# LayerNorm with GELU: giving each partition one stretch of 512 KB in memory instead of 32 KB of every 4 MB block

## The chip, the cores and the metric

One core of one Trainium2 chip runs the kernel; the other cores are idle. The time is the device time in microseconds (us).

## The reference

`x` is 8 x 1024 x 2048 float32: 8192 rows of 2048 numbers, 8 KB a row, 64 MB in all. The output has the same size.

```python
mean = np.mean(x, axis=-1, keepdims=True)
var = np.var(x, axis=-1, keepdims=True)
out = gamma * ((x - mean) / np.sqrt(var + eps)) + beta
return 0.5 * out * (1 + np.tanh(np.sqrt(2 / np.pi) * (out + 0.044715 * out ** 3)))
```

Every row is handled by itself, so any row may be given to any partition, as long as its result is stored in the row it came from.

## The kernel before

The rows are cut into B = 16 blocks of 4 MB. A block gives each of the 128 partitions R = 4 rows, 32 KB. Five slots in SBUF hold a block each; the result is written over the input in its slot and stored from there.

```python
R = 4
SLOTS = 5
SPLIT = 3
...
xg = xf.rearrange("(b p r) d -> b p r d", p=P, r=R)     # block, partition, row
og = of.rearrange("(b p r) d -> b p r d", p=P, r=R)
...
@block.sync                                              # loads
def _(sy):
    for b in range(B):
        s = slot(b)
        if stored(b):
            sy.wait_ge(s_store[s], stored(b))            # the slot's last store has landed
        for q in range(R):
            if b == 0:                                   # blocks 0 and SPLIT: four loads of 1 MB
                sy.dma_start(out=xts[s][:, q:q + 1], in_=xg[0, :, q:q + 1]).then_inc(s_first[q], 16)
            elif b == SPLIT:
                sy.dma_start(out=xts[s][:, q:q + 1], in_=xg[b, :, q:q + 1]).then_inc(s_load[s], 16)
        if b not in (0, SPLIT):
            sy.dma_start(out=xts[s], in_=xg[b]).then_inc(s_load[s], 16 * R)
...                                                      # in the scalar engine's loop over rows:
    if by_row(b):                                        # the last block is stored row by row
        ...
        ac.dma_start(out=og[b, :, q:q + 1], in_=xt[:, q:q + 1])...
    elif q == R - 1:
        ins.then_inc(s_r, 1)
        ac.dma_start(out=og[b], in_=xt)._wait_ge(s_r, b + 1).then_inc(s_store[slot(b)], 16)
```

VectorE takes the statistics, GpSimd the reciprocal root, ScalarE the scaling, VectorE the product with gamma, TensorE adds beta, ScalarE applies GELU.

## Time and profile before

| | before |
|---|---|
| time, median | 320.19 us (320.02 to 320.31, 3 runs) |
| span of the profiled run | 318.5 us |
| bytes moved | 134.26 MB, 421 GB/s on average |
| busiest compute engine (ScalarE) | 79% |
| the two DMA queues together | 98.4% of 16 engines' span |
| 32 KB load packets | 1792, mean 1214.5 ns, 13 of them over 1240 ns |
| 32 KB store packets | 1920, mean 1214.8 ns |

How to read it: the sum of the queue shares says whether the DMA engines have time left, and here they have next to none (98.4%). A share of busy time does not tell whether the engines move data at full pace while they are busy: in one stretch of the changed kernel, shown below, a DMA share of 1.03 stands beside 303 GB/s. For that one looks at the GB/s column of a table of stretches, and at the durations of single packets in the trace. The numbers of packets and their durations in this document are counted from those packet records; a packet is one 32 KB piece of one partition unless its size is given. The table of stretches credits a whole packet to the stretch in which it starts, so in a stretch of 4 us one packet of 32 KB more or less is 8 GB/s.

Two views of before are kept here for later comparison. First, the table of stretches for the 3.7 us before the first store starts, for the 4 us in which the first store ends and the second starts, and for the long middle (columns: window, length, PE, PEld, DVE, ACT, POOL busy, clock, DMA share, GB/s):

```profile
36.00:39.70 3.70, 3.26 (x8) 0.68 (x6) 3.13 (x6) 3.12 (x2) 1.71 (x5) 1.00 1.03 363
53.00:57.00 4.00, 3.27 (x8) 0.70 (x7) 3.43 (x7) 4.00 (x3) 1.63 (x3) 1.00 0.99 426
60.00:260.00 200.00, 160.65 (x349) 37.16 (x348) 165.58 (x262) 165.82 (x88) 74.99 (x132) 1.00 1.00 433
```

Second, the DMA pieces of the chain that ended last, in order of time (start us, us, what):

```profile
68.79 26.55 DMA out_dram<-xt
95.35 33.54 DMA xt<-in_x_dram
...
215.78 35.01 DMA out_dram<-xt
250.80 34.20 DMA xt<-in_x_dram
```

### The profile page before, as it was taken

What the parts mean: (1) busy time and instruction counts of PE and PEld (TensorE: products, weight loads), DVE (VectorE), ACT (ScalarE), POOL (GpSimd) and SP (SyncE); (2) the same over time, 40 slices, a digit from 0 to 9 for tenths busy, and PEclk for the clock granted to TensorE, in tenths of its full rate; (3) what the DMA queues carried; (4) which work ended last, traced back from release to release, by engine and by line L of the source; (5) the groups of instructions that cost most, each with busy time, mean ns of one, the idle gap of its engine ahead of it and who ended that gap; (6) DMA issues with size and microseconds to landing.
All of it is one profiled execution on the core that took longest, in us unless ns stands there. A gap on an engine that the chain in (4) does not pass through costs nothing.

```text
span 318.5 us, 2090 instructions
## 1 busy us (share of the span) xinstructions
PE 244.3 (77%) x520; PEld 57.2 (18%) x520; DVE 247.5 (78%) x386; ACT 251.7 (79%) x132; POOL 110.6 (35%) x201
## 2 busy tenths in 40 slices
PE   2769999999999989687795868958589595886860
PEld 1212222222212112111121112212112121111110
DVE  3499999999999897786968968599686986869810
ACT  2769999999999989698696967969589695995970
POOL 1144444444444444232443333333332433324300
DMA  7999999999999999999999999999999999999995
GB/s 289 438 457 401 394 434 430 444 424 436 432 424 444 417 453 416 440 440 416 457 403 457 420 436 444 411 461 403 453 432 424 449 407 457 424 432 403 453 396 209
DMA packets 6002, 134.26 MB, mean 421 GB/s; under 512 B 704, under 2 KB 752, under 8 KB 752
## 3 DMA queue, kind: packets, MB, share of 16 engines
q1 hardware_dynamic: 3168, 67.11, 49.4%
q10 hardware_dynamic: 2832, 67.13, 49.0%
q14 instruction: 2, 0.02, 0.0%
HBM read 67.13 MB, written 67.11 MB: 421 GB/s over the span
## 4 chain that ended last, share of the span: by engine, by line
DMA 64%; ACT 14%; DVE 10%; POOL 5%; PE 3%; issue 1%; ACTq 0%; DVEq 0%; POOLq 0%; SPq 0%
DMA xt<-in_x_dram 32%; DMA out_dram<-xt 30%; ACT yk L195 9%; DVE sts L149 7%; ACT xt L202 4%; POOL ves L135 3%; DVE zg L158 2%; PE ps L220 2%; DMA rows<-in_gamma_dram 2%; POOL rss L137 2%; POOL nms L139 1%; DVE mvs L155 1%; PE ps L237 1%; ACT g_t L191 1%; ACTq L205 0%
## 5 line engine op out<-in xcount | busy, mean ns | idle before, releaser
L149 DVE BATCH_NORM_STATS2 sts<-xt 128x6 f32<-128x512 f32 x256 | 157.7, 679 | 33.5 <-DMA xt<-in_x_dram 31.9
L195 ACT ACTIVATE yk<-xt,nms,rss 128x2048 bf16<-128x2048 f32 x64 | 133.7, 2090 | 48.9 <-POOL nms L139 42.9
L237 PE MATMUL ps<-zg,ident 128*128 128x512 bf16 x256 | 120.8, 627 | 55.8 <-DVE zg L158 54.7
L233 PE MATMUL ps<-b_hl,ones_b 33*128 33x512 bf16 x256 | 120.6, 624 | 2.2 <-PEq L228 2.2
L202 ACT ACTIVATE xt<-ps 128x2048 f32<-128x2048 f32 x64 | 118.9, 1858 | 1.5 <-PE ps L237 1.5
L135 POOL TENSOR_SCALAR ves<-mvs 128x1 f32<-128x1 f32 x64 | 38.5, 602 | 179.2 <-DVE mvs L155 179.2
L158 DVE TENSOR_TENSOR zg<-yk,g_t 128x2048 bf16<-128x2048 bf16 x64 | 76.5, 1195 | 19.2 <-ACT yk L195 19.2
L237 PEld LDWEIGHTS ps<-zg,ident 128*128 128x128 bf16 x256 | 27.6, 130 | 149.0 <-DVE zg L158 113.7
L233 PEld LDWEIGHTS ps<-b_hl,ones_b 33*128 33x128 bf16 x256 | 27.0, 127 | 92.1 <-issue 88.4
L139 POOL TENSOR_SCALAR nms<-mvs,rss 128x1 f32<-128x1 f32 x64 | 35.7, 558 | 6.3
L137 POOL TENSOR_TENSOR rss<-ves,mhalf 128x1 f32<-128x1 f32 x64 | 35.3, 552 | 5.3
L155 DVE BATCH_NORM_AGGREGATE mvs<-sts 128x2 f32<-128x24 f32 x64 | 16.9, 264 | 2.2
L220 PE MATMUL ps<-rows,ones 1*128 1x512 f32 x8 | 7.2, 1076 | 6.1 <-DMA rows<-in_gamma_dram 6.1
L188 ACT ACTIVATE b_hl<-rows 1x2048 bf16<-1x2048 f32 x1 | 1.9, 1909 | 5.3 <-DMA rows<-in_beta_dram 5.3
L166 DVE TENSOR_TENSOR b_hl<-rows,b_hl 1x2048 bf16<-1x2048 f32 x1 | 2.3, 2280 | 2.8 <-ACT b_hl L189 2.8
L220 PEld LDWEIGHTS ps<-rows,ones 1*128 1x128 f32 x8 | 2.5, 327 | 9.2 <-DMA rows<-in_gamma_dram 6.1
L191 ACT ACTIVATE g_t<-ps 128x2048 bf16<-128x2048 f32 x1 | 1.9, 1877 | 1.9 <-PE ps L220 1.9
L184 ACT ACT_TABLE_LOAD x1 | 1.3, 1283 | 0.9 <-SPq L107 0.9
L189 ACT ACTIVATE b_hl<-rows 1x2048 bf16<-1x2048 f32 x1 | 1.9, 1908 | 0.0
L161 DVE MEMSET b_hl<- 33x1024 uint32 x1 | 0.9, 912 | 1.2 <-SPq L107 1.2
L126 POOL MEMSET ones<- 65x128 f32 x1 | 0.2, 202 | 0.5 <-SPq L107 0.5
L130 POOL TENSOR_SCALAR_AFFINE_SELECT ident<-ident 128x128 bf16<-128x128 bf16 x1 | 0.3, 295 | 0.1
(7 smaller groups left out, 0.9 us busy)
## 6 DMA issues: line engine op xcount, KB each, us to landing
out_dram<-xt ACTq DMA_DIRECT2D x15, 4096.0 KB, 32.6
xt<-in_x_dram SPq DMA_DIRECT2D x14, 4096.0 KB
xt<-in_x_dram SPq DMA_DIRECT2D x8, 1024.0 KB, 8.4
out_dram<-xt ACTq DMA_DIRECT2D x4, 1024.0 KB, 8.6
rows<-in_beta_dram ACTq DMA_DIRECT2D x2, 8.0 KB, 5.9
rows<-in_gamma_dram ACTq DMA_DIRECT2D x1, 8.0 KB, 5.1
```

Source lines behind the costliest of these rows:

```text
L135: po.tensor_scalar(out=ves[:, c], in0=mvs[:, k, 1:2], scalar1=float(eps), scalar2=1.0, op0=ALU.add, op1=ALU.mult)._wait_ge(s_a, k + 1).the ...
L137: po.tensor_tensor(out=rss[:, c], in0=ves[:, c], in1=mhalf, op=ALU.pow)._wait_ge(s_q, 2 * k + 1).then_inc(s_q, 1)
L139: po.tensor_scalar(out=nms[:, c], in0=mvs[:, k, 0:1], scalar1=rss[:, c], scalar2=-1.0, op0=ALU.mult, op1=ALU.mult)._wait_ge(s_q, 2 * k + 2 ...
L149: ins = ve.bn_stats(out=sts[:, q, j, :], in_=xr[:, j, :])
L155: ve.bn_aggr(out=mvs[:, q], in_=sts[:, q])._wait_ge(s_o, count).then_inc(s_a, 1)
L158: ve.tensor_tensor(out=zgs[q % 2], in0=yks[q % 2], in1=g_t, op=ALU.mult)._wait_ge(s_n, count).then_inc(s_z, 1)
L191: ac.activation(out=g_t, in_=pss[0], func=ACT.Identity)._wait_ge(s_tg, 1).then_inc(s_c, 1)
L195: ac.activation(out=yks[t % 2], in_=xts[slot(b)][:, q], func=ACT.Identity, scale=rss[:, q:q + 1], bias=nms[:, q:q + 1])._wait_ge(s_p, t + ...
L202: ins = ac.activation(out=xt[:, q], in_=pss[i % 2], func=ACT.Gelu_apprx_tanh)._wait_ge(s_t, i + 1)
L220: ins = pe.matmul(pss[0][:, cols(j)], lhsT=ones[64:65], rhs=rows[64:65, j * K // nsub:(j + 1) * K // nsub, :d // K], start=True, stop=True)
L233: ins = pe.matmul(ps[:, cols(j)], lhsT=ones_b, rhs=b_hl[:, cols(j)], start=True, stop=False)
L237: ins = pe.matmul(ps[:, cols(j)], lhsT=ident, rhs=zgs[k % 2][:, cols(j)], start=False, stop=True)
```

## The change

Each partition takes one stretch of 64 consecutive rows, 512 KB. Block b is the b-th 32 KB of every stretch. The intent is plain from the pattern: each partition then walks through memory in order. The 128 pieces of one transfer now lie 512 KB apart and not side by side.

```diff
-    xg = xf.rearrange("(b p r) d -> b p r d", p=P, r=R)
-    og = of.rearrange("(b p r) d -> b p r d", p=P, r=R)
+
+    xg = xf.rearrange("(p b r) d -> b p r d", p=P, r=R)
+    og = of.rearrange("(p b r) d -> b p r d", p=P, r=R)
```

## The prediction

> **What bounds the kernel now.** I read the page from its top: the span, the slices, the queue shares. Then the chain that ended last, the waits of the load queue, and a table of stretches.
>
> From the page of the kernel before, span, engine shares, slices and queues:
>
> ```profile
> span 318.5 us, 2090 instructions
> PE 244.3 (77%) x520; PEld 57.2 (18%) x520; DVE 247.5 (78%) x386; ACT 251.7 (79%) x132; POOL 110.6 (35%) x201
> ...
> DMA  7999999999999999999999999999999999999995
> ...
> DMA packets 6002, 134.26 MB, mean 421 GB/s; under 512 B 704, under 2 KB 752, under 8 KB 752
> ...
> q1 hardware_dynamic: 3168, 67.11, 49.4%
> q10 hardware_dynamic: 2832, 67.13, 49.0%
> ```
>
> The reader is to see that no compute engine is over 79% busy, while the DMA digits are 9 from the second slice to the last but one. The two queues (q1 loads, q10 stores) together hold the 16 DMA engines for 49.4 + 49.0 = 98.4% of 318.5 us, that is 313.4 us per engine. The DMA engines have no idle time to give.
>
> The chain that ended last, and the load queue's own waits:
>
> ```profile
> DMA 64%; ACT 14%; DVE 10%; POOL 5%; PE 3%; issue 1%; ACTq 0%; DVEq 0%; POOLq 0%; SPq 0%
> ...
> SPq L122 <- DMA out_dram<-xt: 240.3, 11, 47.2
> ```
>
> The chain is DMA for 64%, loads and stores in turn. The load queue spends 240.3 us waiting for stores to empty a slot: load b+5 goes out when store b lands. So loads and stores form one loop through five slots, and a store that lands late makes a load late. The 36% of the chain put down to compute lies mostly where the engines still have queued packets from other slots: in those stretches the DMA digits are still 9.
>
> The table of stretches (us; the last two columns are the share of the DMA engines' time and the rate):
>
> ```profile
> 20.00:60.00 40.00, 36.14 (x79) 8.25 (x77) 36.99 (x60) 37.46 (x20) 16.61 (x29) 1.00 1.00 421
> 60.00:100.00 40.00, 36.08 (x80) 8.41 (x80) 36.99 (x61) 37.06 (x21) 16.46 (x30) 1.00 1.00 433
> 140.00:180.00 40.00, 30.65 (x67) 6.94 (x65) 31.22 (x49) 31.69 (x18) 14.56 (x27) 1.00 1.00 433
> 220.00:260.00 40.00, 30.59 (x68) 7.14 (x66) 31.50 (x51) 31.58 (x18) 13.73 (x24) 1.00 1.00 432
> 290.00:318.50 28.50, 15.71 (x35) 3.42 (x32) 11.78 (x18) 17.30 (x9) 4.69 (x9) 1.00 0.84 354
> ```
>
> The rate is 432 to 433 GB/s in every middle stretch, whether only loads run (20 to 40 us) or loads and stores together. That flatness is the main reading. The packet records behind it say the same: a 32 KB load packet has a median of 1213 ns (tenth percentile 1213, ninetieth 1218), a 32 KB store packet a median of 1213 and a ninetieth percentile of 1215. 32768 B / 1213 ns = 27.0 GB/s per engine, times 16 is 432 GB/s. A memory that stalls now and then would spread these durations; there is no spread. [...]
>
> [...]
>
> [...]
>
> [...]
>
> [...]
>
> **The change, part by part.** Only the order of the row index differs: partition p's rows in block b were rows b*512 + 4p to b*512 + 4p + 3, and become p*64 + 4b to p*64 + 4b + 3. Same permutation for input and output, and every row is normalised by itself, so the result stays right.
>
> Removed: a 4 MB block that is contiguous in memory (partition pitch 32 KB). Added: a block of 128 pieces of 32 KB at a pitch of 16 blocks x 32 KB = 512 KB. Moved: nothing in SBUF; partition p receives the same 32 KB tile shape in the same slot[...].
>
> Unchanged: the number of packets. Loads: 14 transfers x 128 pieces of 32 KB = 1792, plus 8 x 128 = 1024 of 8 KB. Stores: 15 x 128 = 1920 of 32 KB, plus 4 x 128 = 512 of 8 KB. [...]Issue cost, semaphores, waits and all compute instructions stay too. So instruction costs add 0 us, and the whole question is the duration of a packet.
>
> The sum per engine now. 32 KB packets: (1792 + 1920) / 16 = 232 x 1.215 us (mean of both kinds) = 281.9 us. 8 KB packets: 1024 / 16 x 0.331 + 512 / 16 x 0.314 = 21.2 + 10.0 = 31.2 us. Together 313.1, against 313.4 from the shares. The remaining 5.4 us of the span are the first 1.9 us before a packet starts and the holes of the tail, where the last stores wait for compute (0.84 busy from 290 on: 0.16 x 28.5 = 4.6 us). These are fixed. So span = 5.4 + 313.1 x f, where f is the lengthening of a packet, and the time is the span plus 1.7 us (320.19 against 318.5).
>
> Nothing hides a lengthening: at 98.4% busy it goes to the end nearly in full. One limit on that is the tail: if the memory is slower, compute has more slack, but its holes come after the last load and stay. Slower by 2% is 6.4 us, so f = 1.0205, a 32 KB packet of 1.24 us for 1.215.
>
> **Rivals.** (a) No effect: [...]f = 1.000, time 320. For it: packets without spread[...]. Against it: [...]the flatness promises nothing about another address pattern.
>
> (b) [...]
>
> (c) [...]loads and stores meet: slots put the load about four or five blocks ahead of the store, only 128 to 160 KB within the same partition's stretch, if the two tensors start at like addresses. [...]I give this whole tail, over 340 us, 6%.
>
> (d) One engine slower than the rest: a transfer's semaphore fills when the last of 16 has landed[...].
>
> (e) Faster: packets are at their minimum (1211 ns smallest, 1213 median), and start and tail holes do not depend on addresses. If all 8 KB packets reached a quarter of 1213, 303 ns, that would save 313.1 - 281.9 - 96 x 0.303 = 2.1 us, 0.7%. Faster by 2% cannot be reached: 1%.
>
> **Range and chances.** I weigh (a) with small losses up to 2% at 0.57, (b) and its neighbours from 327 to 340 at 0.36, (c) at 0.06. The median of this lies where a loss of about 1.2% stands: 313.1 x 0.012 = 3.8 us, so 324. The low end is the kernel before less half a microsecond's gain, 319[...]. Faster 0.01, within 2% 0.57, slower 0.42.
>
> **What would show it.** If (a): queue shares again 49.4 and 49.0, middle stretches at 432 to 433 GB/s, 32 KB packets at 1213 ns without spread. If (b): the same counts of packets, shares still near 98 to 99% of a longer span, but [...]a wider spread of packet times; the loads-only stretch from 20 to 40 us tells whether reads alone suffer. If (c): under 400 GB/s where loads and stores overlap. If (d): the DMA share falls below 0.97 in the middle stretches while single packets stay short. In every case compute groups should keep their mean durations (statistics 679 ns, scaling 2090 ns, last activation 1858 ns) and only idle time grow. The prediction is wrong in its ground if packet counts change, if a compute group lengthens, or if the time falls under 314.

The sum came to 5.4 + 313.1 x 1.012 = 322.3 us of span and so to a time of 324 us, with a range of 319 to 336. Terms of it are cut above, since no trace or run of this case shows what they rested on: rival (b), by which every packet is longer (weighed at 327 to 340 us), the high end of the range, which was built on (b), the time that (c) was worked out to, and the cost named for (d). The 1.2% is only the author's estimate, the median of the chances that are given.

## The result, and the profile after

The changed kernel took 324.28 us (median of 4 runs, 323.57 to 324.62) against 320.2 us. Ratio 1.0125, 95% interval 1.0107 to 1.0143. A ratio here is the mean time of one kernel's runs over the mean of the other's of the same rounds, so it is not quite the ratio of the medians. Executions over 1.5% slower than the fastest of the same kernel are left out of the means. In the terms of the prediction this is "within 2%", and it is slower beyond doubt.

From the page after, span and queues:

```profile
span 322.6 us, 2090 instructions
...
q1 hardware_dynamic: 3168, 67.11, 49.7%
q10 hardware_dynamic: 2832, 67.13, 48.4%
```

Same instructions, same packets. The load queue's share rose on a longer span: 0.497 x 322.6 = 160.3 us per engine against 0.494 x 318.5 = 157.3. The store queue's did not: 156.1 us both times. So the loads became slower and the stores did not.

The stretches of after that answer to those shown of before:

```profile
20.00:60.00 40.00, 36.17 (x79) 8.27 (x77) 37.01 (x59) 37.37 (x20) 16.58 (x29) 1.00 1.01 412
60.00:100.00 40.00, 36.12 (x79) 8.38 (x79) 37.02 (x61) 37.10 (x21) 16.46 (x30) 1.00 1.00 429
140.00:180.00 40.00, 30.54 (x67) 7.18 (x68) 31.46 (x50) 31.05 (x17) 13.73 (x25) 1.00 1.00 431
220.00:260.00 40.00, 29.82 (x65) 6.83 (x64) 30.73 (x50) 30.81 (x17) 13.69 (x24) 1.00 1.01 429
290.00:322.60 32.60, 16.70 (x36) 3.84 (x36) 16.29 (x25) 18.45 (x10) 6.52 (x12) 1.00 0.83 352
```

The rate went from 432 or 433 to 429 to 431 GB/s in the middle, and from 421 to 412 between 20 and 60 us. The DMA share stays at 1.00: the engines are as occupied as before and move less. The loss between 20 and 60 us has a place. The same 4 us as above, and the same middle, now of after:

```profile
53.00:57.00 4.00, 3.28 (x9) 0.70 (x8) 3.44 (x7) 3.96 (x3) 1.63 (x4) 1.00 1.03 303
60.00:260.00 200.00, 157.47 (x341) 36.26 (x340) 162.06 (x257) 161.96 (x86) 73.13 (x129) 1.00 1.00 430
```

In the 4 us, 426 became 303 GB/s. The packet records say what fills them: the first store's last packets have just gone out, the second store's first packet comes at 57.1 us, and in between all 16 engines work on loads. Those packets take up to 2755 ns for 1213. Counted over the whole run:

| 32 KB load packets | before | after |
|---|---|---|
| mean | 1214.5 ns | 1240.4 ns |
| median | 1213 ns | 1213 ns |
| over 1240 ns | 13 | 145 |
| before the first store is issued, over 1240 ns | 0 of 256 | 0 of 256 |
| later, with under 2 of 16 engines on stores, over 1240 ns | 0 of 200 | 37 of 62 |
| within 3 us of a handover, over 1240 ns | 1 of 763 | 141 of 720 |
| 32 KB store packets, mean | 1214.8 ns | 1214.6 ns |

(Engines on stores: the mean number of store packets under way while the load packet ran. A packet counts as within 3 us when any part of it is.) So a load packet is not slower in general. A few are slow, where one store ends and the next begins; I call the time from the last packet of one store to the first of the next a handover below, and there are 14 of them. Of all the time that 32 KB load packets take over 1213 ns, 97% lies within 3 us of one: the slow ones between 192 and 196 us, for instance, stand around a store whose last packets end at 193.4 us. The 32 KB loads that start before any store is issued (12 to 31 us) are untouched.

The 8 KB loads just ahead of the first store are not, and in neither kernel. Of the 8 KB load packets that start between 36 us, when the first store is issued, and its first packet at 39.8 us, 33 of 166 take over 400 ns in before and 23 of 178 in after, against a mean of 314 and 313 ns in the 3 us ahead of that. The longest take 840 and 1048 ns, and all the slow ones start in the last 1.5 us. So the kernel before knows this stall too, before any store packet moves; the 363 GB/s of its line for 36.00 to 39.70 above show it, and after has 392 in the same stretch.

The chain of after has the same pieces in the same order, a little later each:

```profile
68.85 28.82 DMA out_dram<-xt
97.69 33.86 DMA xt<-in_x_dram
...
218.91 36.21 DMA out_dram<-xt
255.13 34.41 DMA xt<-in_x_dram
```

The six long DMA pieces of the chain sum to 198.4 us before (26.55 + 33.54 + 34.99 + 34.07 + 35.01 + 34.20) and to 202.8 after (28.82 + 33.86 + 35.00 + 34.52 + 36.21 + 34.41). The 4.4 us are the whole difference of the spans (4.1 us) within the noise of one trace; what follows the last load takes 33.5 us before and 33.1 after.

The 145 slow packets do not explain all of that. All packet time over 16 engines is 313.7 us before and 316.5 after: 2.8 us. The remaining 1.3 us I put down to unevenness; no run isolates it. A transfer is done when the last of its 16 engines has landed, and the trace records each landing. From the first to the last landing of one 4 MB store it is 1.5 us at the first of those I could separate and 2.7 at the most before; after, it grows through the run: 2.1, 2.5, 2.4, 2.5, 2.8, 3.4, 3.9, 4.3, 5.4, 5.5, 5.5, and 1.9 for the last one, when loads are over. Why the landings draw apart is not shown; the trace does not name engines.

### The profile page after: what moved, and what is told of

It reads as the page before. It is cut to its first block, busy times and chain, and to the rows that moved or that the text cites. A ratio compares the mean times of both kernels' runs of the same rounds, so it can differ in the third digit from the quotient of the medians.

```text
span 322.6 us, 2090 instructions
## 1 busy us (share of the span) xinstructions
PE 244.3 (76%) x520; PEld 57.1 (18%) x520; DVE 247.3 (77%) x386; ACT 251.7 (78%) x132; POOL 110.0 (34%) x201
## 2 busy tenths in 40 slices
DMA packets 6002, 134.26 MB, mean 416 GB/s; under 512 B 704, under 2 KB 752, under 8 KB 752
## 4 chain that ended last, share of the span: by engine, by line
DMA 64%; ACT 13%; DVE 10%; POOL 5%; PE 3%; issue 1%; ACTq 0%; DVEq 0%; POOLq 0%; SPq 0%
DMA xt<-in_x_dram 32%; DMA out_dram<-xt 31%; ACT yk L196 8%; DVE sts L150 7%; ACT xt L203 4%; POOL ves L136 3%; DVE zg L159 2%; PE ps L221 2%; DMA rows<-in_gamma_dram 2%; POOL rss L138 2%; POOL nms L140 1%; DVE mvs L156 1%; PE ps L238 1%; ACT g_t L192 1%; ACTq L206 0%
## 5 line engine op out<-in xcount | busy, mean ns | idle before, releaser
L196 ACT ACTIVATE yk<-xt,nms,rss 128x2048 bf16<-128x2048 f32 x64 | 133.7, 2089 | 53.4 <-POOL nms L140 47.4
L203 ACT ACTIVATE xt<-ps 128x2048 f32<-128x2048 f32 x64 | 118.9, 1858 | 1.5 <-PE ps L238 1.5
```

The lines of the kernel that those rows point to most:

```text
L196: ac.activation(out=yks[t % 2], in_=xts[slot(b)][:, q], func=ACT.Identity, scale=rss[:, q:q + 1], bias=nms[:, q:q + 1])._wait_ge(s_p, t + ...
L203: ins = ac.activation(out=xt[:, q], in_=pss[i % 2], func=ACT.Gelu_apprx_tanh)._wait_ge(s_t, i + 1)
```

## The experiments

All three theories that I began with accept the table above and differ in what makes a read slow at a handover. R: strided reads by themselves. W: strided writes, behind which reads wait. C: loads and stores that work in the same stretches, 128 to 160 KB apart. Results first; every row is told below.

| run | time, median us | ratio to before, 95% | slow 32 KB loads | load mean ns | packet time per engine us |
|---|---|---|---|---|---|
| before | 320.2 | 1 | 13 of 1792 | 1214.5 | 313.7 |
| after | 324.28 | 1.0125 (1.0107 to 1.0143) | 145 of 1792 | 1240.4 | 316.5 |
| after_again | 323.19 | 1.0091 (1.0066 to 1.0116) | 134 of 1792 | 1239.5 | 316.4 |
| x_strided | 321.96 | 1.0048 (1.0028 to 1.0068) | 100 of 1792 | 1228.9 | 315.3 |
| out_strided | 321.4 | 1.005 (1.0025 to 1.0076) | 80 of 1792 | 1224.0 | 314.7 |
| pitch256 | 320.75 | 1.003 (1.0005 to 1.0055) | 37 of 1792 | 1215.7 | 314.1 |
| pitch64 | 320.32 | 1.0003 (0.9989 to 1.0016) | 58 of 1792 | 1217.5 | 314.0 |
| pitch504 | 327.87 | 1.0254 (1.0227 to 1.028) | 41 of 1664 | 1217.6 | 314.0 |
| pitch504b | 319.84 | 0.9982 (0.997 to 0.9995) | 8 of 1792 | 1214.8 | 313.2 |

The last three columns belong to the one profiled run of each kernel. Its time was 324.45 us for after, 323.87 for after_again, 323.25 for x_strided, 321.16 for out_strided, 320.19 for pitch256 and 327.71 for pitch504, which is not always near the median. Five more runs (near, near_contig, half_stores and its control, odd_cut) are told below without a row, as their packets or their course differ too much.

### One side at a time: x_strided and out_strided

```diff
 # x_strided: the loads as in the changed kernel, the stores as before
-    og = of.rearrange("(p b r) d -> b p r d", p=P, r=R)
+    og = of.rearrange("(b p r) d -> b p r d", p=P, r=R)
 # out_strided: the other way round
-    xg = xf.rearrange("(p b r) d -> b p r d", p=P, r=R)
+    xg = xf.rearrange("(b p r) d -> b p r d", p=P, r=R)
```

Both put rows in wrong places; their timing is what is wanted.

> Only the loads take the 512 KB pitch; the stores keep the contiguous 4 MB block (the result is wrong on purpose: rows come out permuted). Theory R (strided reads stall by themselves whenever all 16 engines read at once): the full loss, 324 us, some 145 of the 1792 large load packets over 1240 ns, mean near 1240. Theory C (a load and a store collide because both work in the same 512 KB stretches, 128 to 160 KB apart): loads and stores are now in unrelated patterns, so 320 us and under 30 slow load packets. Theory W (scattered writes keep the memory busy and reads behind them wait): 320 us, no slow packets.

> Only the stores take the 512 KB pitch; the loads keep the contiguous block (wrong on purpose). Theory R: 320 us, load packets at 1213 to 1215 ns. Theory C: 320 us. Theory W: the full loss, 324 us, load packets slow in the 2 to 4 us between two stores, store packets still 1213.

Neither expectation came true as written. Each side alone costs about half a per cent, 1.5 us, both together 3 to 4 us. The first handover of each, x_strided and then out_strided:

```profile
53.00:57.00 4.00, 3.27 (x9) 0.70 (x7) 3.43 (x7) 4.00 (x3) 1.63 (x3) 1.00 1.06 377
```

```profile
53.00:57.00 4.00, 3.27 (x8) 0.71 (x7) 3.43 (x6) 3.77 (x3) 1.83 (x4) 1.00 1.07 393
```

377 and 393 GB/s, where before has 426 and the full change 303. The two are only two packets apart. Summed from the packet records, the time over 1213 ns of load packets that start between 50 and 62 us says the same: 0.04 us per engine before, 0.76 and 0.67 with one side strided, 1.33 with both. C falls as the whole cause: with one side strided there are no common stretches, and the stalls are there. R and W fall as sole causes: each side alone brings stalls. What fits is that the pitch of either side makes a read at a handover more likely to wait (100 and 80 slow loads for 13). In out_strided the loads have the very addresses of the kernel before, and 80 of them are slow for 13; so it is not a matter of the read's own address alone. Even then only loads lengthen: the stores' mean is 1214.3 ns.

### A smaller pitch: pitch256 and pitch64

```diff
-    xg = xf.rearrange("(p b r) d -> b p r d", p=P, r=R)
+    xv = xf.rearrange("(g p b r) d -> g b p r d", g=2, p=P, r=R)     # pitch64: g=8
+    xg = [xv[b // 8, b % 8] for b in range(B)]                       # pitch64: b // 2, b % 2
 # and the same for the output
```

> Loads and stores both with half the pitch, 256 KB (two groups of eight blocks; the result is right). If the loss comes from large powers of two between engines and shrinks with the pitch: 321 to 322.5 us, load packets at a mean of 1220 to 1230 ns. If any pitch that is not contiguous costs the same (collision within one stretch[...]): 324 us.

> Pitch 64 KB, eight groups of two blocks, so a transfer spreads over 8 MB and no longer lies in one piece. Power-of-two theory: 320 to 320.5 us, no slow packets, since the kernel before has 32 KB and none. If non-contiguity itself costs: still above 322 us.

The loss falls from 1.25% to 0.3% at half the pitch (320.75 us, less than the 321 to 322.5 expected), and to nothing at 64 KB, which still is no contiguous block. So scattering as such is not what costs. The counts of slow packets do not fall evenly (37 at 256 KB, 58 at 64 KB where none were expected; they are mild, with means of 1215.7 and 1217.5 ns), and the profiled run at 256 KB was one of 320.19 us, without the loss that three of the six runs show (321.23 to 322.56). So I read no law of the pitch from them.

### The same chip for what follows: after_again

No edit; the changed kernel once more.

> The changed kernel once more, on the chip of the three runs beside it, as their yardstick: 1.010 to 1.014 of the kernel before, 323.5 to 324.6 us, load packets with a mean near 1240 ns, store packets at 1215.

1.0091, a little under what was expected, with the same 2.7 us of added packet time (316.4). The first-store handover costs 1.33 us per engine in it, as it did the first time: nearly half of the excess of all 32 KB loads over 1213 ns (2.96 us) lies in one handover of 14.

### Another order of the same stretches: near, and its control near_contig

```diff
 # near: partition 8j+i takes stretch 16i+j, still 512 KB each, still in steps of 32 KB
-    xg = xf.rearrange("(p b r) d -> b p r d", p=P, r=R)
+    xv = xf.rearrange("(i j b r) d -> b j i (r d)", i=8, j=16, r=R)
 # near_contig: the same two-level pattern inside contiguous blocks
+    xv = xf.rearrange("(b i j r) d -> b j i (r d)", i=8, j=16, r=R)
 # and the same for the row-wise loads and for the output
```

> Each partition keeps one 512 KB stretch, in steps of 32 KB, for loads and stores; but stretches are dealt to partitions in another order (partition 8j+i has stretch 16i+j)[...]. Right result. Theory D (what counts is the distance between engines that work at the same moment): nearly as pitch 256, 320 to 321.5 us, under 60 slow load packets. Theory S (what counts is that a partition stays in one stretch and steps by 32 KB, whoever works beside it): 324 us as the changed kernel.

> Control for the run of 423 us: the same two-level address pattern and the same order of partitions, but inside the contiguous 4 MB blocks of the kernel before, so no large power of two in the addresses. If the 423 us came from memory addresses: near 320 us and 430 GB/s in the loads-only stretch. If they came from the way in which a two-level pattern is dealt to the DMA engines[...]: near 420 us, and about 215 GB/s in the loads-only stretch.

Near took 422.82 us, 32% more (1.3158 to 1.324 without the one slow run of six), which no theory of mine had; a stretch of loads alone shows little over half of the 406 GB/s that before has there (near):

```profile
20.00:40.00 20.00, 11.11 (x24) 2.56 (x24) 8.84 (x14) 11.46 (x6) 5.33 (x9) 1.00 1.06 221
```

Taken by itself this run would have looked like a spectacular proof that the addresses are to blame. The control, whose addresses are all inside contiguous blocks, took 423.27 us with the same rate (near_contig):

```profile
20.00:40.00 20.00, 11.12 (x24) 2.58 (x24) 8.96 (x15) 11.46 (x6) 5.33 (x9) 1.00 1.09 227
```

So the large power of two in the addresses has nothing to do with it. Shown is that loads alone ran at 221 and 227 GB/s with this two-level pattern on the memory side, 16 outer and 8 inner, for 406 in before, with addresses far apart or in one block. The reason is not shown: the trace does not name engines. Near therefore says nothing about the change, and the question of which engines' distance matters stays open.

### Closing the handovers: half_stores and before_half_stores

```diff
-                    elif q == R - 1:
+                    elif q % 2 == 1:
                         ins.then_inc(s_r, 1)
-                        ac.dma_start(out=og[b], in_=xt)._wait_ge(s_r, b + 1)...
+                        ac.dma_start(out=og[b, :, q - 1:q + 1], in_=xt[:, q - 1:q + 1])._wait_ge(s_r, 2 * b + (q + 1) // 2)...
 # before_half_stores: the same edit in the kernel before
```

> The changed kernel with each 4 MB store cut into two of 2 MB (16 KB per partition), the first issued two rows earlier, so the store queue should not run dry between two blocks. Theory G (reads stall in the gap of 2 to 4 us when no store is under way and all 16 engines read): gaps gone, slow load packets fall from 145 to under 50, and most of the 4 us comes back: 320.5 to 322 us. If the stalls come from loads and stores being under way together, which this increases: 324 us or more.

> The same cut of the stores in the kernel before, as control: it has no stalls to remove and is at 98 per cent of its DMA engines, so 319.5 to 320.8 us.

A miss: 328.84 us (ratio 1.0252, 1.0229 to 1.0275) and 327.0 us for the control (1.022, 1.0181 to 1.0259; against a mark of 2% that is unclear, but slower it is). Both are slower than what they came from, so the pair doesn't test what it was made for. Slow load packets did not fall to under 50 but rose, to 213, and the control, expected to have no stalls, has 106 of them, many far from its first store; the time over 1213 ns is 4.6 and 2.2 us per engine. The cut also changed how the two queues share the rate: loads run at some 290 GB/s beside stores at 145 (60 to 120 us), which is the ratio of their pieces, 32 and 16 KB. In before, with 32 KB on both sides, it is 216 and 216 (60 to 260 us). One thing is worth keeping from the control. Its first store is issued at 27.8 us, while loads run at full pace, and starts at 33.1 us. The stretches ahead of and within that time (before_half_stores):

```profile
24.00:29.00 5.00, 4.95 (x12) 1.12 (x10) 4.97 (x10) 4.42 (x4) 1.85 (x3) 1.00 0.97 419
29.40:33.00 3.60, 2.88 (x8) 0.73 (x6) 3.04 (x6) 3.60 (x3) 1.62 (x3) 1.00 0.99 282
```

Loads of the contiguous layout fall from 419 to 282 GB/s while a store starts up behind them, with no earlier store anywhere. The stall is therefore not made by the pitch; it exists in the layout of before too. The kernel before itself shows it in the 8 KB loads ahead of its first store (363 GB/s, above), while its first handover is clean (426). That it goes with the start of the store, and not with 8 KB loads as such, the control shows too: its first store starts 6.6 us earlier, and of its 64 load packets of 8 KB that start between 36 and 39.8 us none takes over 309 ns.

### Long stretches without stores: odd_cut

```diff
-                        ac.dma_start(out=og[b], in_=xt)._wait_ge(s_r, b + 1)...
+                        w = P if b % 2 == 0 else 16
+                        ac.dma_start(out=og[b, :w], in_=xt[:w])._wait_ge(s_r, b + 1)...
```

Most rows of odd blocks stay unwritten, so the result is wrong.

> The changed kernel with the stores of odd blocks cut to 16 partitions (wrong on purpose: most rows of odd blocks stay unwritten), so that after each full store follow stretches of loads alone, far longer than the present 2 to 4 us. Theory G1 (at the 512 KB pitch reads stall whenever all 16 engines read, in blocks from the fourth on): slow packets all through those stretches. Theory G2 (reads stall only behind writes that were just made): slow packets within some 4 us of the last store packet and none later. The loads before the first store stay clean under both.

289.68 us, slow packets 311 of 1792. Neither G1 nor G2 holds. Load packets that started in these windows, slow ones of all: 102 to 106 us, 24 of 37; 134 to 138 us, 24 of 40; and between stores, 62 to 66 us, 0 of 57; 96 to 102 us, 0 of 79; 130 to 134 us, 3 of 56. The stalls sit at both ends of the store-free stretches, and the loads in the middle of the early ones run clean at 1213 ns. So it is not "whenever all 16 engines read" (G1), and it is not only behind writes (G2), since the packets at 134 to 138 us come when no store packet had started for 6 us. The store issued at 134.2 us was about to start, with its first packet at 138.8. Later in this run the picture blurs (from 192 to 202 us every window has stalls), and some of its store packets were slow too, up to 5059 ns, which the changed kernel does not show. No such run was made of the layout before.

### No power of two: pitch504 and pitch504b

```diff
 # pitch504: stretches of 63 rows, the last 128 rows one to each partition
-    xg = xf.rearrange("(p b r) d -> b p r d", p=P, r=R)
+    W = T - 1
+    xw = xf[0:P * W].rearrange("(p w) d -> p w d", w=W)
+    xl = xf[P * W:n].rearrange("(p r) d -> p r d", r=1)
 ...
+                    if b == B - 1:                                 # the odd row in the last block
+                        sy.dma_start(out=xts[s][:, :R - 1], in_=xw[:, R * b:W]).then_inc(s_load[s], 16 * (R - 1))
+                        sy.dma_start(out=xts[s][:, R - 1:], in_=xl).then_inc(s_load[s], 16)
 # pitch504b: the odd row in block 0, which is loaded row by row anyway; block b > 0 is
 # xw[:, R * b - 1:R * b + R - 1], and block 0 is stored as 1 MB and 3 MB
 # and the same for the output
```

> Each partition takes a stretch of 63 rows, 504 KB, in the same steps of 32 KB, and one row from the last megabyte; right result. The spread over memory is that of the changed kernel, only the pitch is no power of two. Power-of-two theory[...]: the loss goes away, 319.8 to 321 us (the last block is loaded in two pieces[...]), slow load packets under 40. Spread theory (any blocks scattered over 64 MB read slower beside stores, 4 MB in one piece do not): 323 to 324.5 us, 100 or more slow load packets.

> The 504 KB pitch again, with the odd row moved from the last block to the first one, which is loaded row by row anyway (its store goes out as 1 MB and 3 MB). That takes away the late second load that held up the end of the run before by 7 to 8 us. If power-of-two distances are the cause of the loss: 319.8 to 321 us, under 60 slow load packets, packet time per engine 313.5 to 314.5 us. If the spread over 64 MB costs time by itself: 323 us or more.

Pitch504 came out at 327.87 us, which would count for the spread theory if one looked at the time alone. The stretches tell another story:

```profile
60.00:260.00 200.00, 160.74 (x349) 37.23 (x348) 165.63 (x262) 165.85 (x88) 75.23 (x132) 1.00 1.00 432
...
295.00:304.00 9.00, 4.92 (x11) 1.29 (x12) 8.40 (x15) 4.13 (x3) 3.46 (x6) 1.00 0.02 7
```

Through the middle it runs at 432 GB/s, where before has 433 and after 430, with a load mean of 1217.6 ns and 41 slow packets where under 40 were expected. Its stores are cut and timed as in the changed kernel, so its first handover can be compared:

```profile
53.00:57.00 4.00, 3.27 (x8) 0.70 (x7) 3.43 (x7) 4.00 (x3) 1.63 (x3) 1.00 1.06 451
```

451 GB/s for 426 before and 303 after, and the time over 1213 ns between 50 and 62 us is 0.09 us per engine for 0.04 and 1.33. Over the whole run it is 0.5 us for 0.2 and 3.1. The loss of this run is a hole of 9 us at the end, in which the DMA engines are idle. The second load of the last block, 1 MB in pieces of 8 KB, meets store pieces of 32 KB. Where such pieces meet in before and after (40 to 50 us), the loads move 81 and 78 GB/s and the stores 347 and 351, so the load gets an estimated fifth of the rate. The chain's last load takes 42.2 us for 34.2 before and lands at 294.4 us for 285.0, and the statistics of the last block wait for it. That is my edit's fault, not the pitch's.

Pitch504b mends it. From its page:

```profile
span 318.0 us, 2091 instructions
...
q1 hardware_dynamic: 3168, 67.11, 49.4%
q10 hardware_dynamic: 2976, 67.13, 49.0%
```

319.84 us, 0.9982 of before (0.997 to 0.9995), and 8 slow load packets. The blocks are as scattered over 64 MB as in the changed kernel, in the same steps of 32 KB; the distance between partitions is 504 KB for 512. With that the whole loss is gone. Its spread of landings is steady, 2.4 to 2.7 us to the end. One caution: the first store in two pieces also shifts the handovers in time. Its 3 MB piece is under way until 61.8 us, so this run has no handover at 53 to 57 us at all, and the small gain over before (0.2%) is not put down to the pitch. The first handover and the middle of pitch504 do not have that doubt. Only one pitch that is no power of two was tried.

## Why the prediction was right

The time, 324.28 us, lies beside the predicted 324, inside the range, and in the class that had the largest chance. That it lies so close is in part luck, as the size below shows. The steps one by one:

- **What bounds the kernel, and that nothing hides a longer packet.** Right. The chain's six DMA pieces carry the whole difference, no compute group changed its mean (statistics 678 ns for 679, scaling 2089 for 2090, GELU 1858 for 1858), and the tail behind the last load stayed.
- **The flat rate, "the main reading".** Right for 32 KB packets from 60 us on, wrong for the loads-only stretch and for "there is no spread". The line for 20 to 60 us shows 421 GB/s and not 432, and the same view for 20 to 40 us alone gives 406. The 8 KB load packets of before, which the reading left out, have a median of 309 ns, a mean of 331 and a largest of 1100; 22 of the 231 in the first 7 us take over 400 ns, and 33 of 166 just ahead of the first store.
- **A slip in a sum.** The first 1.9 us and the 4.6 us of holes make 6.5 us, not the 5.4 that are left of the span. It changes little, as the lengthening was applied to the 313.1 us alone.
- **Packet counts and issue costs unchanged.** Right: 6002 packets and 2090 instructions both times.
- **The size, a lengthening of 1.2%.** Right in sum, by the wrong terms. It was drawn as a mixture of "no effect" and rival (b), a lengthening of every packet whose size no run here shows. Measured: packet time per engine rose by 0.9% (316.5 over 313.7), all of it in loads, none of it in stores and none in 8 KB pieces (330 ns for 331). That is 2.8 us of the 4.1; the rest is put down to unevenness between engines, a term the sum did not have.
- **Rival (a), no effect.** True for over 90% of load packets (all but 145 of 1792) and for the stores (mean 1214.6 ns for 1214.8). False for the handovers (303 GB/s for 426 in the first).
- **Rival (b), every packet longer.** Its 327 to 340 us did not come (324.28), nor did the spread of all packets that it named (median 1213 ns both times; 429 to 431 GB/s in the middle). But that the pitch is what costs is shown: 512 KB cost 1.25%, and a pitch 8 KB shorter nothing (0.9982).
- **Rival (c), loads against stores in the same stretches.** Its large loss (over 340 us) did not come, and with one side strided about half of the loss (1.0048 and 1.005) is there without any common stretch.
- **Rival (d), uneven engines.** If the remainder is its work, it is 1.3 us, 0.4%, but the sign named for it was wrong. It was to show in a DMA share under 0.97 in the middle; the share stayed at 1.00. It shows in the spread of the landings, 2.1 us growing to 5.5.
- **That the loads-only stretch would tell whether reads alone suffer.** It did for the 32 KB loads, 0 slow packets of 256, as long as no store was issued. It missed that reads stall just ahead of the first store, in both kernels.

What stays open: why a read waits when a store is about to start or has just ended. Shown are the place of the stalls, that either side's pitch of 512 KB multiplies those at handovers (100 and 80 slow loads for 13), that 504 KB takes nearly all of these away (8 slow loads in pitch504b, 0.09 us per engine at the first handover of pitch504 for 1.33), and that loads stall while a store starts up behind them even in the contiguous layout (282 GB/s for 419). What makes them wait was not shown.

## What to carry to other kernels

In this kernel, bound by DMA (98.4%), changing which rows a partition takes was not free even though every transfer kept its size and shape: a distance of 512 KB between partitions cost 1.25%, 256 KB 0.3%, and 64 KB or 504 KB (63 rows for 64) nothing (1.0003 and 0.9982) against a block in one piece. So when you change such a distance, run a slightly different one beside it. Judge the change by the GB/s in short stretches and by single packets, since the DMA share can hide stalls: here it was 1.03 at 303 GB/s, with packets of up to 2755 ns for 1213. And before you blame addresses, run the same pattern on harmless ones: the run of 422.82 us had nothing to do with large powers of two, as its control took 423.27 without them.
